# One bias table with reversed queries, and the ssm table transfers on GpSimd's queue, in a two-layer attention and state-space trunk

## The chip, the cores and the metric

The kernel runs on one core of one Trainium2 chip. The metric is the device time of one execution in microseconds (us); the profile's times are us from the start of its span unless marked ns. The engines are PE (TensorE), DVE (VectorE), ACT (ScalarE), POOL (GpSimd) and SP (SyncE, which here only issues DMAs).

## What is computed

A trunk of two layers on x, 256 tokens by 1024 channels, all in float32. Each layer is a half-step SwiGLU feed-forward, a token mixer, a second half-step feed-forward and a gated per-layer embedding, each between two RMS norms. The mixer of layer 0 is causal differential attention, that of layer 1 a diagonal state-space model (ssm) with a gated output. Cut to the parts around the change:

```python
def diff_attention(h, w_qkv, w_o, lam_vecs, subln_g, rel_bias, lambda_init):
    ...
        dist = q_pos[:, None] - k_pos[None, :]
        bias = rel_bias.astype(jnp.float32)[t5_bucket(dist)]
        bias = bias.reshape(Q_BLOCK, S, N_HEADS, 2).transpose(2, 3, 0, 1)
        s = jnp.einsum('bhmqd,bhmkd->bhmqk', q_blk, k).astype(jnp.float32) + bias
        s = jnp.where(dist >= 0, s, NEG_INF)
        prob = jax.nn.softmax(s, axis=-1)
        attn = prob[:, :, 0] - lam * prob[:, :, 1]
    ...
def s5_glu(h, lam_re, lam_im, log_dt, b_re, b_im, c_re, c_im, d_skip, w_glu, b_glu):
    ...
    a_bar = jnp.exp(lam_dt)
    b_bar = ((a_bar - 1.0) / lam)[:, :, None] * b
    ...
        y = jnp.einsum('ghp,bcgp->bcgh', c, xs).real + d_g * u_c
    ...
```

The bias depends only on the distance of query and key, for each of the 16 softmax maps (8 heads, two maps each).

## The kernel before

**Tiles and stages.** The tokens are two blocks of 128 (b = 0 and 1), which two generator threads carry through the same stages, block 1 a few steps behind block 0. Weights stream through SP's queue as units of 512 KB, [128, 1024] (class Weights, line 119 issues a load into one of three raw buffers). ACT rounds a unit to its high part (line 131, `hi`), DVE subtracts to get the low part (line 133, `lo`), into nine pairs of buffers. Every product of a unit is three matmuls, hi times hi, lo times hi and hi times lo (function mm3, lines 302 to 304); a unit serves both blocks, so it is worth 12 matmuls of 512 columns. Names in the rows: `up` and `dn` are the accumulators of the feed-forward, `xThi` and `xTlo` its transposed input, `sg` and `h` its activation.

**What sets the order.** A scheduler in the framework fixes the order on every engine when the kernel is built; each engine then runs its own list in that order, and an instruction that waits holds all behind it on its engine. DMAs stand in the list of the engine that issues them.

**The bias table (lines 524 to 540).** At the start POOL fills `tab`, [16 maps, 384], by distance, 32 small copies (line 535). Eight DMAs on SP's queue (line 539) then write 128 copies of it, one per query, to `tab_d` in DRAM, 3.1 MB. In `scores` (lines 580 to 582) each head loads its bias, [128, 2, keys], from `tab_d`: since a copy is 16 x 384 long and the query's step is one less than that, each query's window is shifted by one.

**The ssm tables (function ssm_tables, lines 756 to 967).** While PE works on the feed-forwards and the embedding of layer 0 and on the first feed-forward of layer 1, POOL computes the ssm's matrices group pair by group pair (`vr`, `vi`, then `or`, `oi`, line 894 on), PE transposes them and SP stores them to DRAM (`v_d`, `o_d`). `zt`, a tile of zeros, is written to `m_d` first (line 906); `vr` of the first pair reuses its buffer. At the end, `msb` (the first columns of a Toeplitz matrix) gets the skip connection on its diagonal: four rounds (line 951) load `db` and `dg` (lines 953 and 955, one buffer each), DVE multiplies and adds them (lines 956 to 959); then eight DMAs write `msb` to `m_d` in 1,024 pieces of 64 bytes each (line 962), and eight more copy `m_d`, DRAM to DRAM, to the full Toeplitz rows `t_d` in 1,024 pieces of 512 bytes each (line 965). `t_d` is read in the ssm of layer 1. `V` (line 1243) are stored matrices, loaded early into the space that the tables leave. All these DMAs are issued by SP, between the weight loads. POOL also does the small step of every norm (lines 313 to 317).

Of the kernel before, what the change touches and what calls it, by code (L numbers as in the profile page):

```python
# [9 lines left out]
F32 = mybir.dt.float32  # L10
# [6 lines left out]
P = 128  # L17
# [5 lines left out]
# Places in the schedule, by layer (f01: block 0, second ffn) or by norm (block, norm, token half).  # L23
# [49 lines left out]
def bucket_ranges(n_buckets=32, max_dist=128, n=256):  # L73
    """[start, stop) of the distances in each causal T5 bucket."""
    exact = n_buckets // 2
    of = []
    for d in range(n):
        if d < exact:
            of.append(d)
        else:  # L80
            large = exact + int(math.log(d / exact) / math.log(max_dist / exact) * (n_buckets - exact))
            of.append(min(large, n_buckets - 1))
    return [(of.index(b), n - of[::-1].index(b)) for b in range(n_buckets)]


class Weights:
    """Streams weight tiles [128, 1024] from DRAM and splits each into two float32r parts, or takes two tiles unsplit."""
# [35 lines left out]
    def flush(self, force):  # L123
        """Splits what is loaded, up to the limit."""
        nc = self.nc
        while self.pending and self.pending[0][0] < max(self.split_limit, force + 1):
            n, raw = self.pending.pop(0)
            hi = self.split_pool.tile([P, 1024], F32R, tag="hi", name=f"hi{n}")
            lo = self.split_pool.tile([P, 1024], F32R, tag="lo", name=f"lo{n}")
            with self.hold[0]():  # L130
                nc.scalar.copy(hi, raw)  # L131
            with self.hold[1]():
                (nc.gpsimd if n in self.on_pool else nc.vector).tensor_tensor(lo, raw, hi.bitcast(F32), ALU.subtract)  # L133
            self.tiles[n] = (hi, lo)
# [8 lines left out]
def trunk(ctx, tc, x, p, norm_g, ffn_w_in, ffn_w_out, attn_w_qkv, attn_w_o, attn_lam, attn_subln_g,  # L143
# [17 lines left out]
    def extra_banks(name):  # L161
        """The last two banks serve one section after another."""
        if "cm" in ps_extra:
            ps_extra["cm"].__exit__(None, None, None)
        ps_extra["cm"] = tc.tile_pool(name=name, bufs=1, space=bass.MemoryType.PSUM)
        ps_extra["pool"] = ps_extra["cm"].__enter__()
# [126 lines left out]
    def after_transposes(b, key, left):  # L293
        """The second block's last products of a layer leave room for the first block's transposes of the next."""
        at, step = OPT["at"].get(key, (0, 1))
        n = (at - left) // step + 1 if at else 0
        if b == 0 or n <= 0 or not marks.get(0):
            return nullcontext()
        return tc.issue_after(marks[0][min(2 * n, KT) - 1])
# [62 lines left out]
    def post_norm(b, halves, gain, factor, name):  # L362
        """x += factor * rmsnorm(m) with m in two [128, 512] PSUM banks."""
# [28 lines left out]
    def two_halves(b, accs, hi, lo, units, key):  # L392
        """Products over k into both halves; the last units finish the first half before the second."""
# [122 lines left out]
    if any(st[0] == "attn" for st in stages):  # L516
# [7 lines left out]
        # bias of every softmax map by j = key - query + 127 (distance 255 - j), masked beyond 255  # L524
# [11 lines left out]
        # one copy per query: a stride of one less than a copy then shifts the table by the query  # L536
        tab_d = dram.tile([P, 16, 384], F32, name="tab_d")
        for j in range(8):
            nc.sync.dma_start(tab_d[16 * j:16 * j + 16].rearrange("r m j -> m r j"),
                              tab.rearrange("m (o j) -> m o j", o=1).broadcast_to([16, 16, 384]))  # L540
# [34 lines left out]
    def scores(b, h):  # L575
# [4 lines left out]
        src = tab_d[0, 2 * h:2 * h + 2, 127 + 256 - nk:127 + 256 - nk + 1]  # L580
        nc.sync.dma_start(bias[:, :, 0:nk], bass.AP(tensor=src.tensor, offset=src.offset,
                                                      ap=[[16 * 384 - 1, P], [384, 2], [1, nk]]))
# [34 lines left out]
    def attention(b, qkv_units, pj_units, o_units):  # L617
# [9 lines left out]
        def normed(grp, on):  # L627
# [11 lines left out]
            for h in range(4):  # L639
                nc.tensor.transpose(pt[:, h * P:(h + 1) * P], on[:, h, :], ident)  # L640
            split_T(pt, oT_hi[:, grp * 4:grp * 4 + 4, :].rearrange("p a t -> p (a t)"),
                    oT_lo[:, grp * 4:grp * 4 + 4, :].rearrange("p a t -> p (a t)"), sub_g)
# [8 lines left out]
        for n, (part, grp) in enumerate(QKV_ORDER):  # L651
# [21 lines left out]
            if part == 0:  # L673
                for m in range(2):
                    (nc.vector.tensor_copy if m >= OPT["qz"] else nc.scalar.copy)(
                        qz[b][64 * m:64 * m + 64, :, m, :], ptv[64 * m:64 * m + 64])
            else:
                nc.vector.tensor_copy(kT[:, grp * 4:grp * 4 + 4, b * P:(b + 1) * P], ptv)
                for h in range(grp * 4, grp * 4 + 4):
                    with tc.high_priority(offset=HEAD_OFFSET):  # L680
                        scores(b, h)
                if (2, grp) in QKV_ORDER[:n]:
                    attend_group(grp)
# [34 lines left out]
    def exact_exp(out_, in_, n, nm):  # L718
        """exp to float32 accuracy: 2^(m / 16) times a short series of the rest."""
# [14 lines left out]
    def ssm_exp():  # L734
        """lambda, lambda * dt and the moduli |a|^k with states (e, p) on partitions, columns (q, g'): group 16q + 2g' + e."""
# [20 lines left out]
    def ssm_tables(pool, keep):  # L756
# [7 lines left out]
        # sine and cosine of lambda_im * dt: reduced to [-pi, pi], polynomials of the half angle  # L764
# [24 lines left out]
        # powers of a = rho e^(i theta), then of the phase and of the modulus by squaring  # L789
# [16 lines left out]
        # phases of a^(8j), moduli of a^8  # L806
# [23 lines left out]
        # (a - 1) / lambda  # L830
# [23 lines left out]
        # the norm's gain of the input channels goes into b and d  # L854
# [11 lines left out]
        # output matrices with states on partitions  # L866
# [39 lines left out]
        nc.sync.dma_start(m_d[:, :, 0:7, :].rearrange("i g k o -> i g (k o)"),  # L906
# [42 lines left out]
        # skip connection on the diagonal, Toeplitz rows to DRAM behind seven zero blocks  # L949
        m16 = msb.rearrange("p g e q h -> p (g e q) h")  # L950
        for q in range(4):
            db = pool.tile([16, 16, 16], F32, tag="cn", name=f"db{q}", bufs=1)
            nc.sync.dma_start(db, ssm_d[:, 256 * q:256 * q + 256].rearrange("o (g h) -> o g h", h=16).broadcast_to([16, 16, 16]))
            dg = pool.tile([16, 16, 16], F32, tag="vi", name=f"dg{q}", bufs=1)
            nc.sync.dma_start(dg, norm_g[1, 2:3, 256 * q:256 * q + 256].rearrange("o (g h) -> o g h", h=16).broadcast_to([16, 16, 16]))
# [5 lines left out]
        for k in range(8):  # L961
            nc.sync.dma_start(m_d[:, :, 7 + k, :], m16[16 * k:16 * k + 16])
        yield 2
        for s_ in range(8):
            nc.sync.dma_start(t_d[16 * s_:16 * s_ + 16].rearrange("i g (c x) -> i (g c) x", x=P),
# [4 lines left out]
    def ssm_u(b):  # L970
        """x and the norm's factors to the layout (channel group, block) x (step, channel) through DRAM."""
# [35 lines left out]
    def ssm_core(pool, vs, tos):  # L1007
# [35 lines left out]
        def grouped(out_ap, st_, w, **flags):  # L1043
            """One product per channel group: 32 stationary columns and 128 moving columns each."""
# [288 lines left out]
```

## Time and profile before

| | us |
|---|---|
| median of 3 runs (lowest to highest) | 1148.12 (1147.39 to 1149.25) |
| span of the profiled execution | 1145.0 |
| what lies around the span, by the median | 3.1 |
| PE busy | 1049.3 (92% of the span) |
| DVE busy | 694.8 (61%) |
| ACT busy | 554.4 (48%) |
| POOL busy | 241.3 (21%) |
| mean granted clock of TensorE | 0.965 |

The profiled execution is one of its own, and the page gives its span, from the first instruction to the last. A busy PE is not PE at its peak: matmuls are pipelined. What a stage costs is read from windows of the span (busy time and instruction counts in each) and from the waits in them. DMA-issuing instructions are not counted as busy; SP's work is seen in the timeline of its queue.

### The profile page before, as it was taken

The numbers are of one execution on the slowest core, as the hardware profiler recorded it, in microseconds if no ns is written. First come the engines' busy times: TensorE is split into PE (matmuls) and PEld (weight loads), VectorE is DVE, ScalarE is ACT, GpSimd is POOL, SyncE is SP. The second block draws the span as 40 slices with busy tenths as digits, with TensorE's granted clock in tenths as the row PEclk, the third lists the DMA queues.
The fourth block names the chain that finished last, engine by engine and source line by source line (L and its number), as shares of the span: only waits on it lengthen the run. The fifth ranks groups of instructions, "written<-read, shape, count | busy, mean of one in ns | idle before, by whom it ended". The sixth has DMA issues, their size and how long they took to land.

```text
span 1145.0 us, 14323 instructions
## 1 busy us (share of the span) xinstructions
PE 1049.3 (92%) x5123; PEld 839.2 (73%) x5123; DVE 694.8 (61%) x1011; ACT 554.4 (48%) x873; POOL 241.3 (21%) x289
## 2 busy tenths in 40 slices
PE   6599999999998999999787997999966999999997
PEld 4478888878776787777665776888744878888885
DVE  5166554659838897555678563655358576555464
ACT  5255444556765544443455542544343465444454
POOL 6000000000012004888889400000122010000001
PEclk9799999999999999999998998999987999999999
DMA  8976655646439667666556579756693557564651
GB/s 219 163 246 210 186 189 192 200 145 211 157 128 207 181 192 203 202 206 223 176 165 198 142 204 308 236 200 208 207 358 137 172 178 220 184 186 170 211 168 56
DMA packets 138103, 221.74 MB, mean 194 GB/s; under 512 B 34352, under 2 KB 63024, under 8 KB 138032
## 3 DMA queue, kind: packets, MB, share of 16 engines
q1 hardware_dynamic: 136976, 220.17, 62.8%
q8 instruction: 40, 0.66, 0.2%
q10 hardware_dynamic: 1056, 0.66, 0.2%
q14 instruction: 31, 0.25, 0.1%
HBM read 205.13 MB, written 19.86 MB: 196 GB/s over the span
## 4 chain that ended last, share of the span: by engine, by line
PE 48%; issue 19%; POOL 11%; DMA 9%; DVE 6%; ACT 4%; SPq 3%; DVEq 0%; POOLq 0%; ACTq 0%
PE up L302 7%; PE up L303 7%; PE up L304 7%; DMA raw<-in_ffn_w_in_dram 5%; PE dn L304 4%; PE dn L302 4%; PE dn L303 4%; DVE lo L133 2%; PE qkvat L302 2%; PE qkvat L303 2%; PE qkvat L304 2%; ACT hi L131 2%; POOL or L899 1%; PE sp L586 1%; DMA db<-in_ssm_d_dram 1%
## 5 line engine op out<-in xcount | busy, mean ns | idle before, releaser
L133 DVE TENSOR_TENSOR lo<-raw,hi 128x1024 fp32r<-128x1024 f32 x332 | 425.0, 1286 | 292.3 <-ACT hi L131 289.7
L131 ACT CAST hi<-raw 128x1024 fp32r<-128x1024 f32 x332 | 347.7, 1051 | 349.0 <-DMA raw<-in_ffn_w_in_dram 121.0
L302 PE MATMUL up<-hi,xThi 128*128 128x512 f32 x704 | 281.7, 403 | 22.5 <-ACT sg L444 8.9
L303 PE MATMUL up<-lo,xThi 128*128 128x512 f32 x704 | 280.3, 400 | 2.4 <-DVE lo L133 2.4
L304 PE MATMUL up<-hi,xTlo 128*128 128x512 f32 x704 | 281.6, 405 | 0.0
L302 PEld LDWEIGHTS up<-hi,xThi 128*128 128x128 f32 x704 | 135.5, 193 | 52.8 <-ACT sg L444 9.8
L303 PEld LDWEIGHTS up<-lo,xThi 128*128 128x128 f32 x704 | 135.3, 192 | 33.0 <-DVE lo L133 5.0
L304 PEld LDWEIGHTS up<-hi,xTlo 128*128 128x128 f32 x704 | 135.1, 193 | 29.2 <-issue 0.8
L302 PE MATMUL dn<-hi,hThi 128*128 128x512 f32 x352 | 138.3, 394 | 0.0
L304 PE MATMUL dn<-hi,hTlo 128*128 128x512 f32 x352 | 138.1, 393 | 0.0
L303 PE MATMUL dn<-lo,hThi 128*128 128x512 f32 x352 | 138.0, 392 | 0.0
L313 POOL TENSOR_SCALAR v_pn<-sspn,sspn 128x1 f32<-128x1 f32 x8 | 3.4, 423 | 359.9 <-ACT junkpn L370 356.9
L304 PEld LDWEIGHTS dn<-hi,hTlo 128*128 128x128 f32 x352 | 66.4, 189 | 14.1 <-issue 0.4
L303 PEld LDWEIGHTS dn<-lo,hThi 128*128 128x128 f32 x352 | 66.4, 189 | 13.9 <-DVE lo L133 0.2
L302 PEld LDWEIGHTS dn<-hi,hThi 128*128 128x128 f32 x352 | 66.4, 189 | 13.6 <-issue 0.2
L321 ACT ACTIVATE xThi<-xT_ps,gT 128x128 fp32r<-128x128 f32 x112 | 38.9, 366 | 48.7 <-PE xT_ps L339 48.4
L326 DVE TENSOR_TENSOR hTlo<-hT_ps,hThi 128x512 fp32r<-128x512 f32 (+1 forms) x48 | 30.8, 643 | 36.6 <-ACT hThi L325 36.6
L325 ACT CAST hThi<-hT_ps 128x512 fp32r<-128x512 f32 (+1 forms) x48 | 26.4, 549 | 53.2 <-PE hT_ps L449 53.1
L322 DVE SCALAR_TENSOR_TENSOR xTlo<-xT_ps,gT,xThi 128x128 fp32r<-128x128 f32 x112 | 36.5, 344 | 20.5 <-ACT xThi L321 20.2
L339 PE MATMUL xT_ps<-ident,x 128*128 128x128 f32 x112 | 31.1, 300 | 17.7 <-DVE xTlo L322 10.7
L444 ACT ACTIVATE sg<-up,r_pre 128x512 f32<-128x512 f32 (+1 forms) x48 | 30.8, 650 | 20.9 <-PE up L304 11.5
L446 DVE SCALAR_TENSOR_TENSOR h<-up,r_pre,sg 128x512 f32<-128x512 f32 (+1 forms) x48 | 33.6, 701 | 11.0 <-ACT sg L444 8.5
(352 smaller groups left out, 1296.4 us busy)
## 6 DMA issues: line engine op xcount, KB each, us to landing
raw<-in_ffn_w_in_dram SPq DMA_DIRECT2D x160, 512.0 KB, 4.4
raw<-in_ffn_w_out_dram SPq DMA_DIRECT2D x88, 512.0 KB, 3.9
raw<-in_attn_w_qkv_dram SPq DMA_DIRECT2D x24, 512.0 KB, 4.3
raw<-in_ffn_w_in_dram SPq DMA_DIRECT2D x32, 256.0 KB, 3.5
raw<-in_ple_w_gate_dram SPq DMA_DIRECT2D x16, 512.0 KB, 4.3
raw<-in_ssm_w_glu_dram SPq DMA_DIRECT2D x16, 512.0 KB, 4.2
gain<-in_norm_g_dram SPq DMA_DIRECT2D x8, 512.0 KB, 4.8
raw<-in_attn_w_o_dram SPq DMA_DIRECT2D x8, 512.0 KB, 4.0
```

Of the source, the lines that this page charges most:

```text
L131: nc.scalar.copy(hi, raw)
L133: (nc.gpsimd if n in self.on_pool else nc.vector).tensor_tensor(lo, raw, hi.bitcast(F32), ALU.subtract)
L302: nc.tensor.matmul(out_ap, st_hi, w_hi, start=start, stop=False)
L303: nc.tensor.matmul(out_ap, st_hi, w_lo, start=False, stop=False)
L304: nc.tensor.matmul(out_ap, st_lo, w_hi, start=False, stop=stop)
L321: return (nc.scalar.activation(hi, psum, AF.Copy, scale=scale).ins, nc.vector.scalar_tensor_tensor(lo, psum, scale, hi.bitcast(F32), ALU.m ...
L322: nc.vector.scalar_tensor_tensor(lo, psum, scale, hi.bitcast(F32), ALU.mult, ALU.subtract).ins)
L325: nc.scalar.copy(hi, psum)
L326: nc.vector.tensor_tensor(lo, psum, hi.bitcast(F32), ALU.subtract)
L339: marks[b].append(nc.tensor.transpose(pt, xb[:, k * P:(k + 1) * P], ident).ins)
L444: nc.scalar.activation(sg[:, :w], gp, AF.Silu, scale=r)
L446: nc.vector.scalar_tensor_tensor(h[:, :w], up_, r, sg[:, :w], ALU.mult, ALU.mult)
```

## The change

The table is written once, [16, 384], by one DMA on POOL's queue. The query's window then starts one element later for each row, so row r of a bias tile belongs to query 127 - r of the block: the queries are reversed when they are copied from PSUM (`ptv[..., ::-1]`), and the outputs are turned back when they are split after their transposes. The zero fill, `db`, `dg`, `m_d` and `t_d` go from SP's queue to POOL's. Comments and docstrings are left out too.

```diff
-        tab_d = dram.tile([P, 16, 384], F32, name="tab_d")
-        for j in range(8):
-            nc.sync.dma_start(tab_d[16 * j:16 * j + 16].rearrange("r m j -> m r j"),
-                              tab.rearrange("m (o j) -> m o j", o=1).broadcast_to([16, 16, 384]))
+        tab_d = dram.tile([16, 384], F32, name="tab_d")
+        nc.gpsimd.dma_start(tab_d, tab)
...
-        src = tab_d[0, 2 * h:2 * h + 2, 127 + 256 - nk:127 + 256 - nk + 1]
+        src = tab_d[2 * h:2 * h + 2, 256 - nk:256 - nk + 1]
         nc.sync.dma_start(bias[:, :, 0:nk], bass.AP(tensor=src.tensor, offset=src.offset,
-                                                      ap=[[16 * 384 - 1, P], [384, 2], [1, nk]]))
+                                                      ap=[[1, P], [384, 2], [1, nk]]))
...
-            split_T(pt, oT_hi[:, grp * 4:grp * 4 + 4, :].rearrange("p a t -> p (a t)"),
-                    oT_lo[:, grp * 4:grp * 4 + 4, :].rearrange("p a t -> p (a t)"), sub_g)
+            split_T(pt.rearrange("p (a t) -> p a t", a=4)[:, :, ::-1], oT_hi[:, grp * 4:grp * 4 + 4, :],
+                    oT_lo[:, grp * 4:grp * 4 + 4, :], sub_g)
...
-                        qz[b][64 * m:64 * m + 64, :, m, :], ptv[64 * m:64 * m + 64])
+                        qz[b][64 * m:64 * m + 64, :, m, :], ptv[64 * m:64 * m + 64, :, ::-1])
...
-        nc.sync.dma_start(m_d[:, :, 0:7, :].rearrange("i g k o -> i g (k o)"),
+        nc.gpsimd.dma_start(m_d[:, :, 0:7, :].rearrange("i g k o -> i g (k o)"),
...
-            nc.sync.dma_start(db, ssm_d[:, 256 * q:256 * q + 256].rearrange("o (g h) -> o g h", h=16).broadcast_to([16, 16, 16]))
+            nc.gpsimd.dma_start(db, ssm_d[:, 256 * q:256 * q + 256].rearrange("o (g h) -> o g h", h=16).broadcast_to([16, 16, 16]))
...
-            nc.sync.dma_start(dg, norm_g[1, 2:3, 256 * q:256 * q + 256].rearrange("o (g h) -> o g h", h=16).broadcast_to([16, 16, 16]))
+            nc.gpsimd.dma_start(dg, norm_g[1, 2:3, 256 * q:256 * q + 256].rearrange("o (g h) -> o g h", h=16).broadcast_to([16, 16, 16]))
...
-            nc.sync.dma_start(m_d[:, :, 7 + k, :], m16[16 * k:16 * k + 16])
+            nc.gpsimd.dma_start(m_d[:, :, 7 + k, :], m16[16 * k:16 * k + 16])
...
-            nc.sync.dma_start(t_d[16 * s_:16 * s_ + 16].rearrange("i g (c x) -> i (g c) x", x=P),
+            nc.gpsimd.dma_start(t_d[16 * s_:16 * s_ + 16].rearrange("i g (c x) -> i (g c) x", x=P),
```

Line numbers after line 539 are two lower in the changed kernel (line 962 becomes 960). The order on SP's queue at the start, from the weight loads after the first gain on: before,

```order
L119 DMA raw_308<-in_ffn_w_in_dram 128x2x512
L539 DMA tab_d<-tab 16x16x384 x3
L119 DMA raw_314<-in_ffn_w_in_dram 128x2x512
L539 DMA tab_d<-tab 16x16x384 x2
L119 DMA raw_320<-in_ffn_w_in_dram 128x2x512
L539 DMA tab_d<-tab 16x16x384 x3
L119 DMA raw_407<-in_ffn_w_in_dram 128x2x512
```

and now, from the same weight load (the fourth after the gain) on:

```order
L119 DMA raw_301<-in_ffn_w_in_dram 128x2x512
L119 DMA raw_307<-in_ffn_w_in_dram 128x2x512
L579 DMA bias_0_1918<-tab_d 128x2x128
L579 DMA bias_0_1936<-tab_d 128x2x128
L119 DMA raw_313<-in_ffn_w_in_dram 128x2x512
L579 DMA bias_0_1954<-tab_d 128x2x128
L119 DMA raw_400<-in_ffn_w_in_dram 128x2x512
```

The eight table writes are gone, and the first three bias loads, which stood behind three more weight loads, have moved up to behind the fifth. The order on SP's queue where the ssm tables end, before (`db`, `dg`: the operands of the diagonal; `o_d`: output matrices):

```order
L946 DMA o_d<-oi_4905 64x512 x2
L962 DMA m_d<-msb 1024x1x16 x4
L955 DMA dg_4955<-in_norm_g_dram 16x256
L962 DMA m_d<-msb 1024x1x16 x2
L119 DMA raw_5862<-in_ffn_w_in_dram 128x2x512
L119 DMA raw_5880<-in_ffn_w_in_dram 128x2x512
L955 DMA dg_4962<-in_norm_g_dram 16x256
```

These transfers now stand on POOL's queue, behind POOL's last product of the tables (`oi`) and ahead of its work for the ssm of layer 1 (`zeros`, `ssm_sel`):

```order
L951 DMA db_4946<-in_ssm_d_dram 16x256
L900 TENSOR_TENSOR oi_4898<-oi_4898,pto_4899 128x512
L960 DMA m_d<-msb 1024x1x16 x7
L953 DMA dg_4948<-in_norm_g_dram 16x256
L953 DMA dg_4955<-in_norm_g_dram 16x256
L951 DMA db_4953<-in_ssm_d_dram 16x256
L953 DMA dg_4962<-in_norm_g_dram 16x256
L951 DMA db_4960<-in_ssm_d_dram 16x256
...
L960 DMA m_d<-msb 1024x1x16
L963 DMA t_d<-m_d 1024x128 x8
L1039 MEMSET zeros 1x512
L978 MEMSET ssm_sel 128x128 x2
```

All seven m_d that do not need the diagonal stand ahead of the first `dg`. On DVE the first product of the diagonal stands one split later than before; the order now:

```order
L133 TENSOR_TENSOR lo_5840<-raw_5837,hi_5839 128x1024
L954 TENSOR_TENSOR db_4946<-db_4946,dg_4948 16x256
L955 TENSOR_TENSOR db_4946<-db_4946,ident 16x256
L957 TENSOR_TENSOR msb<-msb,db_4946 16x16x16
L133 TENSOR_TENSOR lo_5858<-raw_5855,hi_5857 128x1024
```

Before, the first of these rows stood behind line 956's product of `db` and `dg`; the splits of the next weights follow it in both. On SP, the four loads of `V` stand 13 weight loads behind the last `o_d` store, and now wait for POOL's transfers out of the tables' buffers.

## Rows read from the trace of the kernel before

**Rows 1.** Windows, first stage; busy us and (instructions) per engine, PEclk, DMA share, GB/s.
```profile
20.00:32.60 12.60, 12.09 (x54) 9.32 (x53) 6.26 (x17) 1.97 (x4) 7.31 (x5) 1.00 0.84 103
32.60:100.00 67.40, 52.05 (x210) 41.64 (x210) 31.21 (x32) 29.57 (x34) 0.00 (x0) 0.85 0.83 215
100.00:120.00 20.00, 20.00 (x94) 16.55 (x93) 11.55 (x12) 10.04 (x12) 0.00 (x0) 1.00 0.62 188
```

**Rows 2.** Timeline of PE; start, duration, ..., [idle before <-releaser], all in us.
```profile
36.95 1.22 PE L302 MATMUL up<-hi,xThi 128*128 128x512 f32 x2 [4.21 <-ACT xThi L321]
55.52 0.80 PE L302 MATMUL up<-hi,xThi 128*128 128x512 f32 x1 [6.83 <-ACT sg L444]
```

**Rows 3.** Timeline of SP's queue, the writes of the bias table.
```profile
20.21 4.22 SPq L539 DMA_DIRECT2D tab_d<-tab  x3
28.37 7.70 SPq L539 DMA_DIRECT2D tab_d<-tab  x2
36.88 8.28 SPq L539 DMA_DIRECT2D tab_d<-tab  x3
```

**Rows 4.** DMA issues of the whole span; then GB/s, 20 to 40 us, 40 slices.
```profile
raw<-in_ffn_w_in_dram SPq DMA_DIRECT2D x160, 512.0 KB, 4.4
tab_d<-tab SPq DMA_DIRECT2D x8, 384.0 KB, 10.1
gain<-in_norm_g_dram SPq DMA_DIRECT2D x8, 512.0 KB, 4.8
dg<-in_norm_g_dram SPq DMA_DIRECT2D x4, 16.0 KB, 3.2
...
GB/s 295 8 98 98 98 98 101 95 95 98 98 98 98 98 95 95 98 98 98 98 98 98 95 98 125 124 281 347 390 263 154 101 117 111 89 109 95 101 95 98
```

**Rows 5.** Windows, while the ssm tables are finished.
```profile
640.00:720.00 80.00, 70.78 (x311) 56.46 (x310) 41.21 (x47) 31.69 (x40) 9.07 (x6) 0.96 0.82 244
```

**Rows 6.** Timeline of SP's queue, the end of the ssm tables.
```profile
650.84 1.16 SPq L946 DMA_DIRECT2D o_d<-oi  x2
655.71 0.86 SPq L955 DMA_DIRECT2D dg<-in_norm_g_dram  x1
684.17 11.52 SPq L965 DMA_DIRECT2D t_d<-m_d  x8
```

**Rows 7.** Timeline of DVE, first diagonal product.
```profile
658.43 0.41 DVE L956 TENSOR_TENSOR db<-db,dg 16x256 f32<-16x256 f32 x1 [5.27 <-DMA dg<-in_norm_g_dram]
```

**Rows 8.** Timelines of ACT and PE, idle for want of weights; the page's L133.
```profile
664.03 1.05 ACT L131 CAST hi<-raw 128x1024 fp32r<-128x1024 f32 x1 [9.98 <-DMA raw<-in_ffn_w_in_dram]
703.72 1.04 ACT L131 CAST hi<-raw 128x1024 fp32r<-128x1024 f32 x1 [10.05 <-DMA raw<-in_ffn_w_in_dram]
...
704.81 0.79 PE L302 MATMUL up<-hi,xThi 128*128 128x512 f32 x1 [6.06 <-ACT hi L131]
...
L133 DVE TENSOR_TENSOR lo<-raw,hi 128x1024 fp32r<-128x1024 f32 x332 | 425.0, 1286 | 292.3 <-ACT hi L131 289.7
```

**Rows 9.** Timeline of POOL, its part in the ssm tables.
```profile
350.93 1.95 POOL L816 COPY rh<-st_r 128x992 f32<-128x992 f32 x1 [3.33 <-DVE st_r L801]
...
444.73 1.11 POOL L897 TENSOR_TENSOR vr<-ar,br 128x512 f32<-128x512 f32 x1 [3.86 <-DMA m_d<-zt]
...
643.17 2.10 POOL L900 TENSOR_TENSOR oi<-ai,cre 128x512 f32<-128x512 f32 x1
...
648.66 2.16 POOL L902 TENSOR_TENSOR oi<-oi,pto 128x512 f32<-128x512 f32 x1
...
814.61 0.36 POOL L980 MEMSET ssm_sel<- 128x128 f32 x2 [129.86 <-PE dn L304]
```

**Rows 10.** Line L962; xcount, then ns min/median/max, first and last start.
```profile
L962 SPq DMA_DIRECT2D m_d<-msb x8: 564/684/1132, 649.4 to 680.6; - x8
```

**Rows 11.** Tiles oT_hi and bias, columns as above.
```profile
L322 DVE SCALAR_TENSOR_TENSOR oT_hi<-oT_psat,sub_g,oT_hi x2: 742/746/751, 307.5 to 327.6; 128x512 fp32r<-128x512 f32 x2
...
L589 DVE TENSOR_TENSOR s<-sp,bias x16: 401/548/694, 256.4 to 309.8; 128x256 f32<-128x256 f32 x8, 128x512 f32<-128x512 f32 x8
```

## The prediction

> **What bounds the kernel now.** I read the busy time by windows first. In steady stretches TensorE (PE) is the bound: 94 PE instructions in 20 us, never idle, clock 1.00 [rows 1], so one instruction is worth 20 / 94 = 0.213 us. Two stages fall short of that rate, and the change touches both.
>
> *First stage.* From 20 to 32.6 us PE runs at the full rate; from 32.6 to 100 us it executes 210 instructions in 67.4 us, and the mean granted clock is 0.85 of the upper level, 2.4 GHz [rows 1]. At the steady rate 210 would take 44.7 us, so 22.7 us are lost. The waits on PE show where: 4.21 and 6.83 us, put down to ACT, which itself had no weights [rows 2]. SP's queue tells why: between 20.2 and 45.2 us the eight writes of the bias table take 4.22 + 7.70 + 8.28 = 20.2 us of issue time, with only two weight loads between them [rows 3]. Each write takes 10.1 us to land against 4.4 us for a larger weight load, and the transfers move at some 98 GB/s while they run [rows 4]. That is 3.1 MB, or 32 us at that rate. PE then starts each time at the lower clock level.
>
> *Second stage.* From 640 to 720 us PE executes 311 instructions in 80 us [rows 5]; at 0.213 us that is 66.2 us of work, 13.8 us lost. SP's queue holds the table transfers among the weight loads: eight m_d and eight small db/dg loads, then t_d, 11.52 us of issue in one piece [rows 6]. DVE stands 5.27 us for a dg load [rows 7], and with it every split of a weight (L133) behind it. ACT twice sits about 10 us without weights; the first gap stops PE at no single place that the waits name, the second costs PE 6.06 us [rows 8].
>
> **The change, part by part.**
>
> *One table instead of 128.* The eight writes go from SP's queue and from the DMA rings; one write of 24 KB comes in. The first three bias loads now stand in SP's queue behind the fifth weight load after the gain and wait for it, with weight loads behind them. POOL has filled the table by about 20 us and the write is small, like dg, 3.2 us to landing [rows 4]; so SP stands some 3 to 5 us. Cover: PE ran to 32.6 us on seven units, and the eighth is now loaded before the bias. I take 20 us of the 22.7 and leave one unit (12 products, 2.6 us) for that wait. Ends: at least the two named waits, 11.0 us; at most 22.7.
>
> *Bias loads from overlapping rows.* All 128 queries now read the same few KB. The gain load reads one 4 KB row 128 times and lands in 4.8 us for 512 KB [rows 4], so I price this at nothing; DVE adds 16 biases from 256.4 to 309.8 us, one per 3.6 us [rows 11], with three buffers, so even 9 us to landing would be hidden.
>
> *Reversed reads.* The query copies and the output splits read PSUM backwards. I price this at nothing; if the step halved the rate, two splits per block of 0.75 us [rows 11] lie before the output projection, under 3 us in all. A gain is excluded: same elements.
>
> *Zero fill on POOL.* POOL now prepares this transfer itself before vi and vr of the first group; vr already waited 3.86 us for its landing [rows 9]. I add one preparation, 2.0 us (below); ends -3.9 (the whole wait gone) and +4.
>
> *The price that decides: g, what POOL needs to issue one transfer of 1,024 pieces.* No POOL transfer is in this trace. The nearest rows: SP issues the same transfer in 0.56 to 1.13 us [rows 10], the low end. If POOL makes the pieces one by one at the pace of its copy, 992 elements in 1.95 us [rows 9], 1,024 cost 2.0 us; at the pace of its two-input operation, 512 in 2.10 us [rows 9], 4.2 us; with one entry for the read and one for the write, 8.4 us, the high end. I take 2.0, because an address list is written, not computed from two inputs.
> The Trainium skill (DMA: Bandwidth & Descriptors, section "Anatomy of one DMA — SWDGE (gpsimd) path") says many descriptors can be emitted before their generation shows and that most of a fixed 2 us is the receipt of the write; by that g lies at the low end and the sum would be near 1118. No row here shows it.
>
> *Table transfers on POOL.* POOL's last product ends at t0 = 648.66 + 2.16 = 650.8 [rows 9]. Behind it now stand seven m_d, then the first dg. So dg is issued at t0 + 7g and lands 3.2 us later [rows 4]. DVE's product of it stands behind one more split; that weight is issued after SP's o_d stores, t0 + 1.2 [rows 6], and needs 4.4 us to land [rows 4], 1.05 for ACT and 1.29 for DVE [rows 8]: DVE arrives at t0 + 7.9. It waits 7g - 4.7 us: 9.3 us at g = 2.0, against 5.27 now. PE's cover is what is split ahead: the gap of 10.05 us cost 6.06, the one of 9.98 nothing that is named [rows 8], so 4 to 10 us; I take 7, and PE loses 2.3. For the three later rounds (POOL, landing, DVE, POOL again) and for the t_d and V traffic, whose bytes do not change, I leave 6 us, the size of the idle after today's t_d. Loss after: 8.3 us; gain 13.8 - 8.3 = 5.5.
> V on SP now waits for the last m_d; behind it stand weight loads. SP comes to it after 13 units of 2.6 us, about t0 + 35; the last m_d lands at about t0 + 7g + 3.2 + three rounds of 5 + g + 3.5 = t0 + 38 (the rounds an estimate from the 3.2 us landing). Three us, within the cover. The eight t_d need 8g more; POOL is next wanted at 814.6 [rows 9], t0 + 163.8, so up to g = 8.4 they stay hidden.
>
> *Sum.* -20 - 5.5 + 2 = -23.5 us. The profiled execution spans 1145.0 us, 3.1 below the median of the runs shown, 1148.1; I take the 3.1 around the span as unchanged: span 1121.5, time **1124.6**.
>
> **Rivals.**
> 1. *POOL's preparation is slow (slower than before).* Seven m_d stand before the first dg, and DVE with all splits waits for that. At g = 8.4: wait 54.1, less 7 of cover, plus 6, less today's 13.8 = +39.3; zero fill +4; first stage -20: +23, **1171**. It decides from g about 5.2, where the three terms cancel. For it: it is software work, and POOL's two-input operations need 4.2 ns an element. Against: a list of addresses needs no operand. Chance 0.16.
> 2. *Middle price.* g = 4.2: wait 24.7 - 7 + 6 - 13.8 = +9.9, zero fill +3, -20: -7, **1141**. It also comes about from g = 2.0 if DVE's work shuts POOL out while it runs: DVE is busy 41.2 of 80 us in this stage [rows 5], so 2.0 becomes 4.1. Chance 0.15.
> The Trainium skill (SBUF — State Buffer, section "Who interferes with whom") has such a lock for DVE's two-port copies and says tensor_tensor, which L133 is, has no such mode. By it the lock would be rare here; no row shows either.
> 3. *The first stage gives only its named waits*, because weights then come no faster than they are landed and split: -11 - 5.5 + 2: **1134**. Against: 188 GB/s suffices at 100 us [rows 1], and slices without table writes reach 390 [rows 4]. Chance 0.13.
> 4. *POOL's queue behaves as SP's does*, g = 0.6, so the move only takes work off SP: DVE waits no longer than now, 13.8 - 6 = 7.8 gained, zero fill 0.6, first stage 22.7: **1118**. Chance 0.12.
>
> **How the numbers follow.** The forecast, 1124.6, has 0.44 (its own range 1118 to 1131). About 0.2% is what a measurement of this kernel can tell from no change: 2.3 us. All cases but the first rival are faster, 0.84; the middle price reaches into no change and beyond at its upper end, so faster 0.80, same 0.04, slower 0.16. The range starts at 1112, where all 22.7 + 13.8 are recovered, and reaches 1152, past the middle price; the slow rival is left out.
>
> **What would show it.** Right: no PE wait over 3 us between 30 and 80 us, clock 1.00 there, about 300 PE instructions done by 80 us; m_d on POOL about 2 us apart; DVE's first diagonal product with about 9 us of idle before it; SP without t_d, weights without a gap of 10 us. Wrong, on the slow side: m_d spaced by 5 us or more, DVE idle over 30 us there, PE idle right after. If the first stage still shows ACT waiting for weights past 35 us, the table write was not its cause. If POOL's preparation is short and PE still loses over 10 us from 640 to 720, the traffic and not the queue was the cost.

## The result, and the profile after

| | before | changed |
|---|---|---|
| time, median us | 1148.68 (1147.39 to 1149.78, 4 runs) | 1130.49 (1129.81 to 1132.92, 4 runs) |
| ratio, 95% interval | | 0.9846 (0.9826 to 0.9865) |
| profiled execution: time, span us | span 1145.0 | 1130.13, span 1128.3 |

The change makes the kernel 18.2 us faster; 23.5 were forecast. The time lies in the range (1112 to 1152), a wide one, and the sign is right. The parts of the sum are less so.

Windows of the changed kernel, one core: busy us and (instructions) of PE, PEld, DVE, ACT, POOL, then PEclk, DMA share, GB/s.

```profile
32.60:80.00 47.40, 41.93 (x180) 33.87 (x180) 26.88 (x29) 24.29 (x27) 0.00 (x0) 0.93 0.65 196
44.50:48.70 4.20, 4.20 (x11) 3.26 (x10) 3.44 (x5) 2.82 (x3) 0.00 (x0) 0.50 0.54 150
640.00:720.00 80.00, 73.52 (x328) 59.79 (x327) 43.12 (x51) 34.23 (x40) 10.84 (x18) 0.96 0.80 255
```

At the 0.213 us that one PE instruction is worth in a steady stretch [rows 1], the first row is 38.3 us of work in 47.4: 9.1 us lost (9.9 up to 100 us, where 270 instructions are done; there before lost 22.7 [rows 1]). The last row is 69.9 us of work in 80: 10.1 lost, against 13.8 [rows 5].

Where the first 9.1 us go, from the timelines of PE and ACT:

```profile
43.87 0.79 PE L302 MATMUL up<-hi,xThi 128*128 128x512 f32 x1 [5.33 <-ACT sg L444]
44.46 0.63 PE L303 MATMUL up<-lo,xThi 128*128 128x512 f32 x1
44.89 0.63 PE L304 MATMUL up<-hi,xTlo 128*128 128x512 f32 x1
...
49.09 0.40 PE L302 MATMUL up<-hi,xThi 128*128 128x512 f32 x1
49.32 0.39 PE L303 MATMUL up<-lo,xThi 128*128 128x512 f32 x1
```

```profile
37.32 1.06 ACT L131 CAST hi<-raw 128x1024 fp32r<-128x1024 f32 x1 [0.24 <-DMA raw<-in_ffn_w_in_dram]
40.77 1.04 ACT L131 CAST hi<-raw 128x1024 fp32r<-128x1024 f32 x1 [2.39 <-DMA raw<-in_ffn_w_in_dram]
41.83 1.28 ACT L444 ACT_TABLE_LOAD   x1
43.13 1.27 ACT L444 ACTIVATE sg<-up,r_pre 128x512 f32<-128x512 f32 x2
```

PE stands once, 5.33 us, for a Silu (sg) that frees a PSUM bank. That Silu stands on ACT behind a cast that waits 2.39 us for a weight, and behind a table load of 1.28 us. After the gap PE runs at the lower clock level, 1.2 GHz (granted clock 0.50 from 44.5 to 48.7 us, the second row): products start 0.43 us apart instead of 0.23 for 12 products, 2.4 us. Together 7.7 of the 9.1.

Of the two waits of before [rows 2], the one of 6.83 us was put down to the same Silu line, but it has another cause. In the timeline of ACT before:

```profile
54.77 0.69 ACT L444 ACTIVATE sg<-up,r_pre 128x512 f32<-128x512 f32 x1 [7.83 <-DMA tab_d<-tab]
```

The table `tab` (line 532) and `sg` (line 443) have the same tag in a pool of two buffers, so this Silu could not write its result until the last of the eight table writes out of `tab` had landed: it was issued at 41.1 us and took 13.5.

Where the 10.1 us go: the timelines of POOL, DVE, ACT and PE in the second stage, then a window.

```profile
634.79 5.32 POOL L960 DMA_DIRECT2D m_d<-msb  x7
640.60 0.50 POOL L953 DMA_DIRECT2D dg<-in_norm_g_dram  x1 [0.49 <-issue]
...
669.72 0.77 POOL L960 DMA_DIRECT2D m_d<-msb  x1 [5.93 <-DVE msb L957]
673.66 6.04 POOL L963 DMA_DIRECT2D t_d<-m_d  x8 [3.17 <-DMA m_d<-msb]
```

```profile
647.80 0.41 DVE L954 TENSOR_TENSOR db<-db,dg 16x256 f32<-16x256 f32 x1 [1.46 <-DMA dg<-in_norm_g_dram]
...
693.46 1.23 DVE L133 TENSOR_TENSOR lo<-raw,hi 128x1024 fp32r<-128x1024 f32 x1 [13.10 <-ACT hi L131]
```

```profile
692.39 1.04 ACT L131 CAST hi<-raw 128x1024 fp32r<-128x1024 f32 x1 [12.74 <-DMA raw<-in_ffn_w_in_dram]
```

```profile
693.48 0.80 PE L302 MATMUL up<-hi,xThi 128*128 128x512 f32 x1 [5.62 <-ACT hi L131]
```

```profile
680.00:700.00 20.00, 13.92 (x55) 10.75 (x54) 3.76 (x5) 4.03 (x5) 0.20 (x1) 0.83 0.92 335
```

DVE's wait for the first dg fell from 5.27 [rows 7] to 1.46 us. The gap after t_d is still there, though SP's queue no longer holds t_d: ACT waits 12.74 us for a weight (10.05 before [rows 8]), and DVE 13.10 behind it. PE executes 55 instructions in 680 to 700 us where 94 fit: 8.3 us, nearly all that is lost in this stage.

These are the numbers of one execution. In a second one of the same kernel (e12 below) ACT's gap is 9.29 us, PE's 2.12 instead of 5.62, and the stage loses 7.9 us instead of 10.1:

```profile
640.00:720.00 80.00, 76.29 (x339) 61.88 (x339) 42.78 (x51) 34.63 (x41) 14.36 (x22) 0.98 0.79 257
```

The price that decided, by line (xcount, ns min/median/max), and the transfers (KB each, median us from issue to landing):

```profile
L960 POOL DMA_DIRECT2D m_d<-msb x8: 763/785/806, 634.8 to 669.7; - x8
L963 POOL DMA_DIRECT2D t_d<-m_d x8: 759/759/774, 673.7 to 678.9; - x8
```

```profile
t_d<-m_d POOLq DMA_DIRECT2D x8, 512.0 KB, 14.2
V<-v_d SPq DMA_DIRECT2D x4, 512.0 KB, 10.5
m_d<-msb POOLq DMA_DIRECT2D x8, 64.0 KB, 7.2
dg<-in_norm_g_dram POOLq DMA_DIRECT2D x4, 16.0 KB, 3.0
tab_d<-tab POOLq DMA_DIRECT2D x1, 24.0 KB, 2.0
```

POOL issues a transfer of 1,024 pieces in 0.76 to 0.81 us (SP: 0.56 to 1.13, [rows 10]); 2.0 were taken.

One measure serves for all that follows: the times at which ACT starts the squares of the residual norms (junkpn, 32 in the program, the same in every kernel). Us by which a square starts earlier than before, from one profiled execution each:

| square (before at, us) | 1st (215.8) | 8th (363.5) | 16th (618.8) | 17th (813.9) | 32nd (1138.5) | median us, ratio (95%) |
|---|---|---|---|---|---|---|
| changed | 13.2 | 13.4 | 11.7 | 16.3 | 16.8 | 1130.49, 0.9846 (0.9826 to 0.9865) |
| e1 one table alone | 13.7 | 13.8 | 13.2 | 13.0 | 13.5 | 1132.68, 0.9871 (0.9854 to 0.9888) |
| e2 queue alone | -1.7 | -1.6 | -8.3 | -0.9 | 1.4 | 1144.10, 0.9965 (0.9951 to 0.9978) |
| e3 bias loads on GpSimd | 13.5 | 13.5 | 9.2 | 16.3 | 16.7 | 1129.38, 0.9829 (0.9806 to 0.9851) |
| e4 t_d paced | 13.5 | 14.9 | 10.1 | 23.9 | 27.2 | 1123.06, 0.9776 (0.9756 to 0.9796) |
| e5 128 copies from GpSimd | -2.4 | -2.9 | -3.7 | -3.7 | -3.0 | 1149.52, 1.0004 (0.9985 to 1.0022) |
| e7 Silu first | 20.7 | 21.0 | 19.1 | 26.6 | 28.3 | 1125.43, 0.9800 (0.9773 to 0.9827) |
| e8 t_d paced, zero fill on SP | 12.9 | 13.7 | 12.4 | 25.0 | 26.7 | 1120.80, 0.9745 (0.9720 to 0.9771) |
| e9 t_d paced, Silu first | 21.2 | 22.7 | 16.6 | 29.3 | 30.0 | 1115.63, 0.9712 (0.9685 to 0.9739) |
| e12 changed, again | 14.6 | 14.4 | 7.8 | 15.1 | 17.0 | 1127.15, 0.9810 (0.9789 to 0.9831) |
| e11 zero fill on SP | 13.8 | 14.3 | 12.9 | 20.9 | 23.0 | 1125.25, 0.9793 (0.9772 to 0.9815) |
| e10 all three | 20.7 | 22.5 | 21.7 | 34.9 | 36.3 | 1112.47, 0.9682 (0.9661 to 0.9704) |

e1 to e4 share a chip and its runs of the kernel before (1147.67), e5 to e9 a second (1149.19), e10 to e12 a third (1149.26). The changed kernel itself gave 1130.49 and, with e10 and e11, 1127.15, so two or three us between kernels of different chips say nothing. Nor do one or two us between squares of single executions: the changed kernel's first square came at 202.5 us in one and at 201.2 in the other.

### The profile page after: what moved, and what is told of

Its sections match the earlier page's. It is cut to its first block, busy times and chain, and to the rows that moved or that the text cites. A ratio compares the mean times of both kernels' runs of the same rounds, so it can differ in the third digit from the quotient of the medians.

```text
span 1128.3 us, 14341 instructions
## 1 busy us (share of the span) xinstructions
PE 1044.2 (93%) x5123; PEld 836.1 (74%) x5123; DVE 694.4 (62%) x1011; ACT 553.4 (49%) x873; POOL 258.9 (23%) x315
## 3 DMA queue, kind: packets, MB, share of 16 engines
q0 software_dynamic: 1824, 5.33, 1.8%
## 5 line engine op out<-in xcount | busy, mean ns | idle before, releaser
L133 DVE TENSOR_TENSOR lo<-raw,hi 128x1024 fp32r<-128x1024 f32 x332 | 427.5, 1294 | 271.1 <-ACT hi L131 269.4
L304 PEld LDWEIGHTS up<-hi,xTlo 128*128 128x128 f32 x704 | 134.0, 191 | 29.3 <-issue 0.6
L304 PEld LDWEIGHTS dn<-hi,hTlo 128*128 128x128 f32 x352 | 66.4, 189 | 14.2 <-issue 0.2
L303 PEld LDWEIGHTS dn<-lo,hThi 128*128 128x128 f32 x352 | 66.4, 189 | 13.4
L321 ACT ACTIVATE xThi<-xT_ps,gT 128x128 fp32r<-128x128 f32 x112 | 38.7, 367 | 50.3 <-PE xT_ps L339 50.0
L302 PE MATMUL qkvat<-hi,xThi 128*128 128x512 f32 x96 | 38.1, 397 | 0.2 <-ACT xThi L321 0.2
```

The costliest lines, as they stand in the source:

```text
L302: nc.tensor.matmul(out_ap, st_hi, w_hi, start=start, stop=False)
L303: nc.tensor.matmul(out_ap, st_hi, w_lo, start=False, stop=False)
L304: nc.tensor.matmul(out_ap, st_lo, w_hi, start=False, stop=stop)
L321: return (nc.scalar.activation(hi, psum, AF.Copy, scale=scale).ins, nc.vector.scalar_tensor_tensor(lo, psum, scale, hi.bitcast(F32), ALU.m ...
```

## The experiments

**e1 and e2: each half alone.** e1 is the changed kernel with this edit (the same for db, dg, m_d and t_d); e2 is the kernel before with it reversed.

```diff
-        nc.gpsimd.dma_start(m_d[:, :, 0:7, :].rearrange("i g k o -> i g (k o)"),
+        nc.sync.dma_start(m_d[:, :, 0:7, :].rearrange("i g k o -> i g (k o)"),
...
```

> The change with its second part taken back: one bias table, reversed queries, the table written from GpSimd's queue, but zero fill, db/dg, m_d and t_d issued from SyncE as before. Theory (the two parts add up): the first stage keeps its whole gain, 13 us by the square of the first residual (215.8 to 202.5 us), and the second stage keeps its old loss, so about 1148.7 - 13 = 1135.5 us, and the fifth junkpn group (813.9 us before) at about 801. Rival A (the table is all that matters, the queue is worth nothing): as the change, 1130.5. Rival B (the parts need each other, SyncE stands longer for the table transfers once the first stage is faster): over 1139.

> The change with its first part taken back: 128 copies of the bias table written from SyncE as before, but zero fill, db/dg, m_d and t_d issued from GpSimd. Theory: nothing changes up to 430 us; from 620 to 810 us some 4.8 us are gained, of which the stretch from 540 to 620 may give back up to 2: 1143.5 to 1146 us. Rival A (the queue is worth nothing, the 4.8 us came from what the shift by 13 us did to the order): within 1.5 us of before. Rival B (GpSimd's transfers land later, 7.2 us against 3.5, and DVE waits for them): over 1150.

e1: 1132.68, 15.0 us under before, between the two numbers expected; its squares settle it, 13.7 us at the first and 13.0 at the 17th, so the second stage keeps its old loss. e2: 1144.10, 3.6 us under before. The time is in its theory's range, the parts are not: it loses 6.7 us from the 8th to the 16th square (up to 2 were expected) and wins 7.4 from there to the 17th (4.8). The two halves add up to the whole: 15.0 + 3.6 = 18.6 against 18.2.

**e5: the table's bytes or SP's queue?** The kernel before, with one edit:

```diff
-            nc.sync.dma_start(tab_d[16 * j:16 * j + 16].rearrange("r m j -> m r j"),
+            nc.gpsimd.dma_start(tab_d[16 * j:16 * j + 16].rearrange("r m j -> m r j"),
```

> The kernel before with one edit: the eight writes of the 128 copies of the bias table are issued from GpSimd's queue instead of SyncE's; the bytes (3.1 MB) stay. Theory (in the first stage the table's bytes on the DMA engines cost, each write 10.1 us to landing): weights still land late, PE keeps gaps of together over 8 us between 30 and 90 us, the first residual square at 211 us or later (215.8 before, 202.5 in the change), time 1143 or more. Rival (the issue time in SyncE's queue, 20.2 us, costs): the first residual square at 202 to 205 us, time 1133 to 1138.

1149.52, no change. The timelines of POOL and PE, and the windows of e5:

```profile
22.87 2.50 POOL L539 DMA_DIRECT2D tab_d<-tab  x4
25.39 0.59 POOL L317 TENSOR_TENSOR r_pre<-v_pre,neg_half 128x1 f32<-128x1 f32 x1
25.93 2.26 POOL L539 DMA_DIRECT2D tab_d<-tab  x4
```

```profile
59.46 0.80 PE L302 MATMUL up<-hi,xThi 128*128 128x512 f32 x1 [21.61 <-ACT sg L444]
```

```profile
40.00:50.00 10.00, 0.00 (x0) 0.00 (x0) 1.33 (x2) 1.04 (x1) 0.00 (x0) 0.56 1.01 149
```

SP's queue is free, POOL issues all eight writes in 4.8 us, and PE still loses 21.6 us in one piece while the DMA engines are full (DMA share 1.01). So taking the issue off SP's queue gives nothing while the writes stay: the cost is their work on the DMA engines, and SP's 20.2 us of issue [rows 3] were its sign. Whether it is the bytes or the number of pieces no run tells: the engines are full here at 149 GB/s. Nor is it shown what SP's issue time would cost with writes that don't come all at once (here they land in 19.0 us instead of 10.1), or what part of e1's 15.0 us is the buffer that `tab` shares with `sg`: no run gives `tab` one of its own.

**e3: is the rest of the first stage SP's wait for the table?** On the changed kernel, for the three bias loads that wait for it:

```diff
-        nc.sync.dma_start(bias[:, :, 0:nk], bass.AP(tensor=src.tensor, offset=src.offset,
+        (nc.gpsimd if b == 0 and h < 3 else nc.sync).dma_start(bias[:, :, 0:nk], bass.AP(tensor=src.tensor, offset=src.offset,
```

> The changed kernel with the first three bias loads, which wait for the table, issued from GpSimd's queue behind the table's write, so that SyncE's queue holds nothing but weights in the first 60 us. Theory (what is left of the first stage's loss is SyncE's wait of 3.5 us for the table: PE's gap of 5.33 us before 43.87 us and the 12 products at the lower clock level behind it, 12 x 0.2 = 2.4 us): no PE gap over 1 us between 30 and 60 us, 5 to 8 us faster than the changed kernel, 1122.5 to 1125.5. Rival (weights are landed and split no faster than this anyhow, and the gap is the activation table load on ACT): the gap stays at 3 us or more and the time within 2 us of the changed kernel's 1130.5.

The theory falls. SP issues nothing but weights (33 of them) from 10.1 to 99.2 us, and PE's gap stays, in the timeline of e3:

```profile
43.55 0.79 PE L302 MATMUL up<-hi,xThi 128*128 128x512 f32 x1 [5.53 <-ACT sg L444]
```

The first square comes 0.3 us earlier than in the change. The rival's time holds; which cause keeps the gap is open after this run.

**e7: the place of the Silu on ACT.** On the changed kernel, an order on ACT alone: the casts of the weight units 10 to 12 come after the first Silu. Behind the Silu of the feed-forward's loop (put_behind adds the order of one cast behind it):

```diff
+            silu = nc.scalar.activation(sg[:, :w], gp, AF.Silu, scale=r)
+            if (b, i, f, c) == (0, 0, 0, 0):
+                for n_ in range(10, 13):
+                    W.behind[n_] = silu
+                    if n_ in W.casts:
+                        W.put_behind(n_)
```

> The changed kernel with one order on ACT: the first Silu, which frees a PSUM bank for PE's next product and loads ACT's table (1.28 us), goes ahead of three casts of weights, of which the last waits 2.39 us for its load. Theory (what is left of the first stage's loss is this order: PE's gap of 5.33 us before 43.87 us ends with that Silu, plus 2.4 us at the lower clock level): no PE gap over 2 us between 30 and 60 us, the first residual square at 195 to 198 us (202.5 in the change), time 1123 to 1126. Rival (the weights come no faster, SyncE's three raw buffers bound them): the gap comes back as a wait on a cast or a split within the next 10 us, first residual square after 200.5 us, time within 2 us of 1130.5.

1125.43, and the first square at 195.1 us, 7.4 earlier than in the change and 6.1 earlier than in its second execution (e12). The timeline of ACT and the windows of e7:

```profile
34.83 1.05 ACT L133 CAST hi<-raw 128x1024 fp32r<-128x1024 f32 x1 [1.58 <-DMA raw<-in_ffn_w_in_dram]
35.90 1.28 ACT L453 ACT_TABLE_LOAD   x1
37.20 0.69 ACT L453 ACTIVATE sg<-up,r_pre 128x512 f32<-128x512 f32 x1
```

```profile
32.60:80.00 47.40, 46.90 (x214) 38.38 (x213) 31.21 (x33) 28.19 (x34) 0.00 (x0) 1.00 0.75 229
```

214 instructions instead of 180, no gap, and clock 1.00. ACT still waits for weights (5.39 us before 31.68), but PE has enough in hand. So the weights came fast enough; the order on ACT held the bank.
The Trainium skill (ScalarE: Activation LUTs, section "What ACT_TABLE_LOAD costs") gives 1283 ns for such a load; the trace agrees, with 1.28 us. The load stands right before the first Silu in both kernels, in PE's gap in the changed one and behind work that PE has in hand in e7.

**e4: traffic or queue in the second stage?** The changed kernel; before each t_d transfer POOL reads one element of a weight unit, each time two units further on, so that the eight go out at the weights' pace. The copy's result is not used.

```diff
...
+        n = min(flat(plan[("ffn", 1, 0)])) + 33 + 2 * (8 - len(toeplitz))
+        if n in W.tiles:
+            s_ = toeplitz.pop(0)
...
+            seen = nc.gpsimd.tensor_copy(pc, W.tiles[n][0].bitcast(F32)[0:1, 0:1])
+            with tc.issue_after(seen.ins):
+                nc.gpsimd.dma_start(t_d[16 * s_:16 * s_ + 16].rearrange("i g (c x) -> i (g c) x", x=P),
+                                    m_d.rearrange("i g k o -> i g (k o)")[:, :, 16 * s_:16 * s_ + P])
...
```

> The changed kernel with its eight t_d transfers no longer issued in one piece: before each, GpSimd reads one element of a weight tile, of the 34th, 36th, ... unit of that feed-forward layer, so they go out about every 5 us over some 40 us. Theory (traffic: t_d and V, 6.3 MB at some 380 GB/s, starve the weights for 12 to 13 us between 680 and 700): DVE's gap of 13.1 us shrinks under 6, PE loses 3 us or less there instead of 8.3, time 1122 to 1126. Rival A (the loss is V's, or of the wait for m_d in SyncE's queue): the gap stays, within 2 us of 1130.5. Rival B (a t_d transfer costs the weights as much however it is spread): the same loss in several smaller gaps, within 2 us of 1130.5.

1123.06, as the theory said. Its timeline of POOL (first and last of eight), its windows and its transfers:

```profile
695.07 0.78 POOL L1242 DMA_DIRECT2D t_d<-m_d  x1
...
731.80 0.76 POOL L1242 DMA_DIRECT2D t_d<-m_d  x1
```

```profile
640.00:720.00 80.00, 80.00 (x370) 66.29 (x369) 47.26 (x55) 37.68 (x44) 15.43 (x21) 1.00 0.78 250
640.00:760.00 120.00, 120.00 (x552) 99.38 (x551) 69.72 (x78) 57.17 (x67) 21.05 (x27) 1.00 0.77 252
```

```profile
t_d<-m_d POOLq DMA_DIRECT2D x8, 512.0 KB, 6.6
```

PE is never idle through all eight and executes 370 where 328 were (339 in e12); a t_d lands in 6.6 us instead of 14.2. The same bytes from the same queue cost next to nothing when they are spread, so the loss was the burst, t_d in one piece on top of V. Pacing also moves t_d behind V, which is issued at 674 us here, 21 us before the first t_d; what a burst clear of V would cost no run shows. From the 16th to the 17th square e4 wins 13.9 us, as much as the stage had lost before (13.8).

**e8, e11 and e12: the zero fill.** e11 is the changed kernel, e8 is e4, each with the zero fill's line as in e1's diff; e12 is the changed kernel unedited.

> The kernel with the paced t_d transfers (1123.1 us) with the zero fill back on SyncE's queue. Theory (the zero fill on GpSimd, 0.88 us of issue ahead of the table chain, shifts that chain against TensorE's order, so that TensorE waits 3.0 to 4.4 us for vi and for xTlo near 590 us instead of 1.3 to 1.5): the loss of 2 to 5 us between the squares at 363 and at 618 us goes, time 1119 to 1121.5. Rival (the loss there is chance of the order, not the zero fill): within 1.5 us of 1123.1.

> The changed kernel with the zero fill alone back on SyncE's queue. Theory (the zero fill on GpSimd costs about 2 us between the squares at 363 and at 618 us, as the prediction's +2 said): that stretch loses under 1 us, time 1.5 to 2.5 us under the changed kernel run beside it. Rival (what is lost there is given back from 640 to 720 us, where the weights run into t_d and V anyhow): the stretch loses under 1 us, but the time is within 1 us of the changed kernel's.

> The changed kernel once more, unedited, beside the next two on the same chip: 1129 to 1132 us.

The stretch from the 8th to the 16th square can be read in every kernel. With the zero fill on POOL it loses 1.6, 6.7, 4.3, 4.8, 1.9, 6.1 and 6.6 us (changed, e2, e3, e4, e7, e9, e12), with it on SP 0.6, 0.9, 1.3, 1.4 and 0.8 (e1, e5, e8, e11, e10). The first and the last of the seven are the same kernel, 1.6 and 6.6. In the changed kernel PE waits, in its timeline (here one of POOL's products and one of DVE's):

```profile
587.22 0.33 PE L339 MATMUL xT_ps<-ident,x 128*128 128x128 f32 x1 [3.02 <-DVE xTlo L322]
596.76 0.33 PE L921 MATMUL v_ps<-ident,vi 128*128 128x128 f32 x1 [3.42 <-POOL vi L900]
```

and in e11, for the same two:

```profile
585.79 0.33 PE L339 MATMUL xT_ps<-ident,x 128*128 128x128 f32 x1 [1.26 <-DVE xTlo L322]
...
593.04 0.47 PE L921 MATMUL v_ps<-ident,vi 128*128 128x128 f32 x1 [1.46 <-POOL vi L900]
```

Such single waits are not the whole of it. The stretch as one window, in e12 and then in e11:

```profile
349.11:611.02 261.91, 240.63 (x1155) 187.40 (x1153) 182.50 (x295) 125.55 (x189) 157.33 (x133) 0.95 0.62 191
349.16:605.95 256.79, 235.97 (x1153) 184.06 (x1154) 180.73 (x296) 125.85 (x190) 158.62 (x133) 0.98 0.64 197
```

PE is idle for 21.3 us in e12 and 20.8 in e11, nearly the same; it is busy 4.7 us longer with the same work, at a granted clock of 0.95 instead of 0.98. In this stretch the clock is 0.95 to 0.98 in the seven executions with the zero fill on POOL and 0.98 or 0.99 in the five with it on SP. The three that lose over 6 us (e2, e9, e12) are those at 0.95: there the cost is for the most part time at the lower clock level, while in e4 it is PE's idle time, 23.2 us against 19.5 before. Why the clock falls more often, in one execution of a kernel and not in another, is open.

In time the edit is worth 1.9 us (e11 under e12), 2.3 (e8 under e4) and, with e10 below, 3.2 (under e9); only the first pair shares a chip, the intervals overlap in each pair, and the sign agrees in all three. So a gain of about 2 us is likely and not shown. e8 alone would not have suggested it: its last square is no earlier than e4's. Two of the expectations were missed: e11's stretch lost 1.4 us instead of under 1, and e12's 1127.15 is under the 1129 to 1132 expected. What part is the 0.88 us of issue at the head of POOL's chain and what the other order of PE's products that comes with it isn't separated.

**e9 and e10: together.** e9 is e4 with e7's edit, e10 is e9 with the zero fill on SP.

> The paced t_d transfers and the first Silu ahead of three casts, together, on the changed kernel. Theory (independent stages, the gains add): 1123.1 less what the Silu's place gives alone, 1116 to 1118 if that is 5 to 7 us. Rival (the Silu's place gives nothing): 1121 to 1125.

> The changed kernel with all three edits: the first Silu ahead of three casts, the paced t_d transfers, the zero fill on SyncE. Theory (the zero fill's 2 us add to the 1115.6 us of the first two): 1111.5 to 1114.5. Rival (they are given back): 1114.5 to 1117.

e9 took 1115.63, just under the 1116 to 1118 of its theory, and e10 1112.47 us, 0.9682 (0.9661 to 0.9704) of before, the fastest of all: 36.8 us under before and 14.7 under the changed kernel on its chip (e12). The windows of e10:

```profile
32.60:80.00 47.40, 46.88 (x213) 38.52 (x214) 31.34 (x33) 28.30 (x34) 0.00 (x0) 1.00 0.74 231
640.00:720.00 80.00, 80.00 (x367) 66.07 (x366) 49.05 (x57) 38.97 (x44) 18.37 (x24) 1.00 0.81 267
```

At 0.213 us each that is 45.4 us of work in 47.4 and 78.2 in 80: both stages of the prediction now run within about 2 us of the steady rate.

## Why the prediction was right, and where it was off

- **Sign and halves.** The table half was put at -20 and gave -15.0 (e1); the queue half was put at -5.5 + 2 = -3.5 and gave -3.6 (e2). The forecast was off by 5.3 us, 5.0 of it in the first half. That the second agrees so closely is luck: by e2's squares its parts are -7.4 and +6.7.
- **The signs set down beforehand.** Most did not come: PE waited 5.33 us, the clock was 0.93 and 271 instructions were done by 80 us, not 300; m_d went out some 0.78 us apart, not 2; DVE stood 1.46 us, not 9; weights kept a gap of 12.74 us on ACT. One pointed the wrong way: ACT does wait for a weight past 35 us (2.39 us before 40.77), which was to show that the table write was not the cause, and e1 shows that the table is worth 15.0 us.
- **The mis-sized term is "I take 20 us of the 22.7 and leave one unit (12 products, 2.6 us) for that wait".** That wait, SP's for the new table, was there (3.5 us in SP's queue) and cost nothing that e3 could give back. What was left was 9.1 us, of which 6.1 to 7.4 are the Silu's place on ACT (e7). The prediction read both of its named waits as lack of weights; the longer one, 6.83 us "<-ACT sg" [rows 2], was a Silu that waited 7.83 us for `tab`'s buffer, as shown above, and that wait did go with the writes. With the order mended, the first square comes 20.7 to 21.2 us earlier (e7, e9, e10): the 20 us were there to be had, but not by this edit alone.
- **SP's issue time was read as the cost** beside the writes' slow landing. e5 takes the issue alone off SP's queue, and nothing is gained.
- **The third rival** (only the named waits, 1134) came nearer in time, within 3.5 us against 5.9 for the forecast. Its reason does not hold: in e7 the weights come from the same queue and PE has no gap (214 instructions instead of 180).
- **The price g.** Taken 2.0, measured 0.76 to 0.81 us, near the low end of 0.56, and below every price made from POOL's elementwise work. The Trainium skill (DMA: Bandwidth & Descriptors, section "Anatomy of one DMA — SWDGE (gpsimd) path") says that many descriptors can be emitted before the cost of making them shows; the trace bears it out in the main, with 0.76 us for 1,024 pieces against 0.49 for a dg. (The page of the changed kernel counts 1,824 packets for the 26 transfers on POOL's queue, 70 each, so that POOL makes 1,024 entries is not shown.) The slow rival and the middle price fall with that. The fourth rival had the right g and was off by the first stage and by the 6 us left for traffic.
- **The wait for dg.** Forecast 9.3 us, measured 1.46. dg went out 5.8 us after POOL's last product instead of 14, but landed in 7.2 us instead of 3.2, behind seven m_d on the same queue. DVE came 3.6 us later than the 7.9 forecast, too. With 7 x 0.78 + 7.2 = 12.7 against DVE's 11.5, the prediction's own formula gives 1.2.
- **The residual 6 us for "later rounds" and the t_d and V traffic** was 8.3 in 680 to 700 us, almost all traffic. So the loss after, 8.3 forecast and 10.1 measured (7.9 in e12), was nearly right as a sum of wrong parts. "If POOL's preparation is short and PE still loses over 10 us from 640 to 720, the traffic and not the queue was the cost" is what happened in the first execution and nearly so in e12, and e4 bears out the reason.
- **V on SP:** forecast to find m_d done at t0 + 38 and wait 3 us; it was issued at t0 + 38.7 (673.50 - 634.84), 2.6 us after SP's last weight. Its cover held.
- **The zero fill,** +2.0: e11, e8 and e10 give 1.9 to 3.2, none of them clear of noise by itself. The size may be right, the working is not: the issue took 0.88 us, and most of what the stretch loses in e12 is PE's work at a lower clock, not a wait for the fill.
- **Priced at nothing, rightly:** a bias load lands in 4.0 us (median of the 128 KB ones; 4.8 before), the split that reads PSUM backwards takes 746 ns as it did [rows 11], and the query copies 688 ns as before.

## What to carry to other kernels

A queue whose issues take long may only show that the DMA engines are full: move the writes to another queue and the stall moves along with them; shrink them, or spread those that nobody needs soon. A releaser in a row is only the first step back. PE's "<-ACT sg" stood for two things here, a buffer that a DMA still read and a cast that stood ahead of the Silu, and each goes by another edit; follow such a wait on the engine that it names, and price it by itself. A transfer that nobody needs for 100 us is best issued at the pace of the work beside it, not when its input is ready.

## What the runs showed of the hardware that was not expected

- POOL's issue of a transfer did not grow when the transfers landed late: e5's eight writes of 384 KB were issued in 4.8 us and landed in 19.0 us (median); on SP the same eight took 20.2 us to issue [rows 3].
- Seven m_d in a row land later from POOL's queue, 5.0 to 8.3 us (SP: 3.2 to 4.2 before, 3.3 to 4.0 in e1), with the same bytes. The eighth, issued by itself, takes 3.7 us from POOL and 3.5 from SP, and the zero fill, 448 KB, 7.5 and 7.4. So it is the row of them and not a single transfer that is slower; why is open.
- Between the 17th and the 32nd square, a stretch that the edits don't touch, the profiled executions still gain between 0.4 us (e3) and 3.3 (e4). All are held against one execution of the kernel before, which may be a slow one there; this was not looked into.
